# One hybrid attention layer on one core: the transposes of the differential heads' values write to another PSUM pool

## The chip, the core and the metric

The kernel runs on one core of a Trainium2 chip. The metric is the device time of one execution in microseconds (us). The engines are named as the profile names them: PE (matrix products and transposes), PEld (its weight loads), DVE (vector), ACT (scalar), POOL and SP (which only issues DMAs here). Each takes its own instructions strictly in the order of the program and waits at semaphores for the others. The granted clock of PE was 0.996 of full speed over the profiled execution, which is the 2.4 GHz level throughout.

## What is computed

One decoder layer on 1024 tokens of 1024 features. The input is normalised and projected by one matrix whose columns feed two groups of heads; their gated outputs are concatenated, projected, normalised and added to the input. Cut to what matters here:

```python
h = rmsnorm(x, ln_pre_g)
q_nope, q_rope, c_kv, k_rope, g_a, dq, dk, dv, g_b = split(h @ w_in)
# group A: 4 heads over a shared latent c_kv (normalised, then up-projected to keys and values)
o_a = causal_attention(q_a, k_a, v_a, 192 ** -0.5) * silu(g_a)
# group B: 4 differential heads; dq, dk are two maps of 64, dv is 128 wide
a1 = causal_attention(rope(dq)[..., 0, :], rope(dk)[..., 0, :], dv, 64 ** -0.5)
a2 = causal_attention(rope(dq)[..., 1, :], rope(dk)[..., 1, :], dv, 64 ** -0.5)
o_b = rmsnorm(a1 - lam * a2, subln_g) * (1 - lambda_init) * silu(g_b)
x = x + rmsnorm(concat(o_a, o_b) @ w_out, ln_post_g)
```

The projections are made transposed (features on partitions, 512 tokens at a time). The attention needs the values with tokens on partitions, so each head's values are transposed back after their projection. That step is what the change touches.

## The kernel before

Every fp32 product is split in a high and a low half and done in three passes (high by high, high by low, low by high).

The **projection** of one 128-column tile for 512 tokens is 24 matrix products of 512 columns (L512) into one bank of the pool `psj` (tile name `j`, two banks), over eight slices of the input `xh`, `xl` with weights `wh`, `wl`. `ORDER` (L952) lists which tile comes when: for the differential heads the gates `gb`, keys `dk`, queries `dq` and values `dv`, then the latent `c`, the shared rotary key `kr` and the rest. After each tile a generator takes the result out of its bank: `ev_g`, `ev_dk`, `ev_dq`, `ev_c`, and `ev_dv` for the values. Rotary tiles leave the bank by two DVE instructions (L263, a shuffle, and L264). The latent `c` keeps its bank through a long chain: ACT copy, transposes (L283), squares, a power on POOL, a scaling on DVE (L292 to L300), transposes back (L309) and the last evictions (L310, L311).

The **attention** of one head and one pair of query blocks is two stages. `stage1` makes the scores (L698) in 512-column pieces in the pool `pss` (tile `s`, two banks), and DVE copies each piece out, masks it and takes its minimum (L704); ACT makes the exponentials (L711). For the differential heads the two maps are combined by DVE (L729, odd query blocks) or by ACT and POOL (L733, L734, even ones). `stage2` transposes the probabilities on PE (L761) into the pool `pst` (tile `t`, two banks), splits them in two halves by ACT (L111) and DVE (L112) and multiplies them with the values (L774, L779) into `pso` (tile `o`, two banks). `finish_b` normalises a head's output (L819 to L839, among them L833 on PE).

Sets of the two stages are merged with the projection: after each piece of attention, `pump` lets the projection's generator run for a share of that time, so the projection's products fill PE while DVE and ACT work on scores. This gives the order in which the work is written. The Tile framework then puts each engine's instructions in a static order of its own, from that order, the dependencies and the banks: the banks of a pool go round in the order in which the tiles are asked for, and a tile can be written only when the tile two before it in its pool has been read for the last time. So two things tie PE to DVE: a score piece waits for L704 of the piece two before, and a projection tile waits for the last read of the tile two before.

`ev_dv` for heads 1 to 3 (head 0's call has `have_r=False`, made at the start from the first products): DVE scales the bank into `e` (L424); after a pause of two steps four PE transposes (L435) write `e` back into the same bank `ps`; ACT and DVE then split that bank into `dvh` and `dvl` (L437, recorded under the helper's lines L111 and L112). The bank of `psj` is thus held until the second of these has read it. For head 0 the transposes already go to a bank of `pst`.

Of the kernel before, what the change touches and what calls it, by code (L numbers as in the profile page):

```python
# [8 lines left out]
F32 = mybir.dt.float32  # L9
# [7 lines left out]
P = 128  # L17
# [34 lines left out]
def hybrid_layer_kernel(  # L52
# [29 lines left out]
    pst = ctx.enter_context(tc.tile_pool(name="pst", bufs=2, space=PSUM))  # L82
# [27 lines left out]
    def split(hi, lo, src, eng=None):  # L110
        nc.scalar.copy(hi, src)  # L111
        (eng or nc.vector).tensor_tensor(lo, src, hi.bitcast(F32), op=ALU.subtract)  # L112
# [305 lines left out]
    def ev_dv(ps, n, h, have_r=True):  # L418
        cs = slice(n * 512, (n + 1) * 512)
        if n == 0:  # L420
            state["dv", h] = hin.get("dvh"), hin.get("dvl")
        if have_r:
            e = tp.tile([P, 512], F32, tag="e", name="e")
            nc.vector.tensor_tensor(e, ps, R[:, cs], op=ALU.mult)  # L424
        else:
            slot = hin.get("dve", F32)
            hin.put(slot)
            e = slot[0][:, 0:512]
            nc.scalar.copy(e, ps)
            yield  # L430
            nc.vector.tensor_tensor(e, e, R[:, cs], op=ALU.mult)
        yield
        pt = ps if have_r else pst.tile([P, 512], F32, tag="t", name="t")
        for j in range(4):
            nc.tensor.transpose(pt[:, j * P : (j + 1) * P], e[:, j * P : (j + 1) * P], ident)  # L435
        v = state["dv", h]
        split(v[0][0][:, cs], v[1][0][:, cs], pt)  # L437


    evict = {  # L440
        "c": (ev_c, 4), "kr": (ev_kr, 2), "qn": (ev_qn, 2), "qr": (ev_qr, 2), "ga": (ev_g, 0),
        "dk": (ev_dk, 4), "dq": (ev_dq, 2), "dv": (ev_dv, 2), "gb": (ev_g, 0),
    }
    ready = set()
# [218 lines left out]

    tab = load_tables(1)
    gens = [ev_dv(acc[2][n], n, 0, False) for n in range(2)]
    for n in range(2):
        next(gens[n])
# [385 lines left out]
```

## Time and profile before

| | us |
|---|---|
| median of three runs | 598.85 |
| lowest, highest | 598.53, 599.79 |
| the profiled execution | 598.69 |
| its span, first to last instruction | 596.6 |
| outside the span | 2.1 |
| busy in the span: PE | 582.9 (98%) |
| busy in the span: DVE | 352.8 (59%) |
| busy in the span: ACT | 299.9 (50%) |
| busy in the span: POOL | 264.0 (44%) |

A share of the span hides that DVE is used unevenly. From 260 to 290 us it is busy for 28.3 us of 30, and from 310 to 320 us for 2.7 of 10. A busy PE isn't a PE at its peak either: a product's record is longer than the distance to the next, since they overlap.

### The profile page before, as it was taken

The page shows a single profiled execution, that of the slowest core. Times are in us where ns is not written, and L with a number is a line of the kernel's source. Part 1 is how long each engine was busy: PE and PEld are TensorE (multiplying, and loading weights), DVE is VectorE, ACT ScalarE, POOL GpSimd, SP SyncE. Part 2 cuts the span into 40 slices and gives each one's busy share as a digit, 9 for nine tenths or more (in the row PEclk, how much of TensorE's full clock was granted, in tenths as well). Part 3 has the DMA queues.
Part 4 walks back from the last instruction along what each step waited for, and adds up shares of the span by engine and source line. Part 5 has one row for each costly group of instructions (what it writes and reads, how often), then busy time and mean ns, then how long its engine had stood idle before and what let it go on. Part 6 is the DMA issues. An engine that isn't in the chain of part 4 may idle for free.

```text
span 596.6 us, 9022 instructions
## 1 busy us (share of the span) xinstructions
PE 582.9 (98%) x3072; PEld 494.8 (83%) x3072; DVE 352.8 (59%) x893; ACT 299.9 (50%) x682; POOL 264.0 (44%) x246
## 2 busy tenths in 40 slices
PE   8999999999999999999999999999999999999995
PEld 5887888788788888887888888888888878888885
DVE  4459566865678585789963555454346477345232
ACT  5743445555555544577643555454445875333111
POOL 2455884393685769538856222014310870000000
PEclk9999999999999999999999999999999999999998
DMA  8943981144041545201125110012403541443223
GB/s 291 404 147 86 215 230 46 44 117 105 26 107 35 131 111 158 63 27 45 47 60 124 37 53 19 34 47 66 113 27 107 169 144 45 139 155 109 70 71 106
DMA packets 39901, 61.60 MB, mean 103 GB/s; under 512 B 4784, under 2 KB 17328, under 8 KB 39856
## 3 DMA queue, kind: packets, MB, share of 16 engines
q1 hardware_dynamic: 39712, 61.03, 34.7%
q8 instruction: 24, 0.39, 0.3%
q14 instruction: 21, 0.17, 0.1%
q10 hardware_dynamic: 144, 0.01, 0.0%
HBM read 38.47 MB, written 7.86 MB: 78 GB/s over the span
## 4 chain that ended last, share of the span: by engine, by line
PE 81%; DVE 8%; DMA 5%; issue 2%; ACT 2%; POOL 1%; SPq 1%; DVEq 0%; POOLq 0%; ACTq 0%
PE j L512 40%; PE j L599 15%; PE s L698 11%; PE o L774 6%; PE t L761 5%; DMA xn<-in_x_dram 2%; DMA xr<-in_xT_dram 1%; DVE pr L704 1%; DMA wor<-in_wout_dram 1%; PE o L779 1%; PE j L358 1%; DMA wf<-in_w_dram 1%; PE j L492 1%; PE o L806 1%; DVE pl L112 1%
## 5 line engine op out<-in xcount | busy, mean ns | idle before, releaser
L512 PE MATMUL j<-xh,wh 128*128 128x512 f32 x368 | 147.2, 400 | 1.6 <-DVE e L264 0.9
L512 PE MATMUL j<-xl,wh 128*128 128x512 f32 x368 | 145.4, 395 | 0.0
L512 PE MATMUL j<-xh,wl 128*128 128x512 f32 x368 | 145.4, 395 | 0.0
L711 ACT ACTIVATE pr<-pr,st 128x128 f32<-128x128 f32 (+7 forms) x96 | 74.5, 776 | 71.2 <-DVE st L704 65.3
L129 POOL TENSOR_TENSOR wl<-wr,wh 128x512 fp32r<-128x512 f32 x48 | 63.4, 1320 | 70.1 <-ACT wh L128 70.1
L512 PEld LDWEIGHTS j<-xh,wh 128*128 128x128 f32 x368 | 69.3, 188 | 14.2 <-DVE e L264 1.3
L512 PEld LDWEIGHTS j<-xh,wl 128*128 128x128 f32 x368 | 69.2, 188 | 13.0
L512 PEld LDWEIGHTS j<-xl,wh 128*128 128x128 f32 x368 | 69.3, 188 | 11.8
L704 DVE CUSTOM_DVE_ANT_0 pr<-s,mask 128x512 f32<-128x512 f32 (+3 forms) x96 | 54.2, 569 | 34.3 <-PE s L698 30.2
L112 DVE TENSOR_TENSOR pl<-t,ph 128x512 fp32r<-128x512 f32 (+1 forms) x80 | 45.5, 578 | 20.0 <-ACT ph L111 19.1
L111 ACT CAST ph<-t 128x512 fp32r<-128x512 f32 (+1 forms) x80 | 38.5, 495 | 29.7 <-PE t L761 29.5
L761 PE MATMUL t<-ident,pr 128*128 128x128 f32 x288 | 48.2, 273 | 1.9 <-DVE pr L729 1.5
L599 PE MATMUL j<-woh,mh 128*128 128x512 f32 (+1 forms) x119 | 45.5, 384 | 0.0
L599 PE MATMUL j<-wol,mh 128*128 128x512 f32 (+1 forms) x119 | 45.1, 379 | 0.0
L599 PE MATMUL j<-woh,ml 128*128 128x512 f32 (+1 forms) x119 | 44.9, 379 | 0.1
L128 ACT CAST wh<-wr 128x512 fp32r<-128x512 f32 x48 | 29.6, 617 | 25.3 <-PE j L512 17.0
L761 PEld LDWEIGHTS t<-ident,pr 128*128 128x128 f32 x288 | 35.6, 141 | 7.6 <-ACT dvh L111 1.3
L108 POOL TENSOR_TENSOR q<-q,nhalf 128x1 f32<-128x1 f32 x8 | 4.4, 552 | 82.7 <-DVE q L610 82.7
L704 DVE CUSTOM_DVE_ANT_0 pr<-s,mask,st 128x256 f32<-128x256 f32 (+2 forms) x48 | 27.8, 580 | 16.2 <-PE s L698 14.8
L698 PE MATMUL s<-dkh,dq 128*128 128x512 f32 (+2 forms) x96 | 34.7, 363 | 0.8 <-DVE st L704 0.6
L265 POOL TENSOR_TENSOR sw<-sw,sr 128x512 f32<-128x512 f32 x18 | 23.2, 1291 | 23.6 <-DVE sw L263 23.5
L698 PE MATMUL s<-dkl,dq 128*128 128x512 f32 (+2 forms) x96 | 32.7, 342 | 0.0
(218 smaller groups left out, 1296.7 us busy)
## 6 DMA issues: line engine op xcount, KB each, us to landing
wr<-in_wt_dram SPq DMA_DIRECT2D x50, 256.0 KB, 2.7
xn<-in_x_dram SPq DMA_DIRECT2D x8, 512.0 KB, 9.6
dkh<-kh SPq DMA_DIRECT2D x32, 128.0 KB, 2.6
dkl<-kl SPq DMA_DIRECT2D x32, 128.0 KB, 2.6
wor<-in_wout_dram SPq DMA_DIRECT2D x16, 256.0 KB, 3.2
xn<-in_x_dram SPq DMA_DIRECT2D x16, 256.0 KB, 3.9
xr<-in_xT_dram SPq DMA_DIRECT2D x7, 512.0 KB, 6.8
scratch<-og SPq DMA_DIRECT2D x28, 128.0 KB, 1.8
```

Of the source, the lines that this page charges most:

```text
L111: nc.scalar.copy(hi, src)
L112: (eng or nc.vector).tensor_tensor(lo, src, hi.bitcast(F32), op=ALU.subtract)
L128: nc.scalar.copy(wh[:, :w], raw[:, :w])
L129: (eng or nc.gpsimd).tensor_tensor(wl[:, :w], raw[:, :w], wh[:, :w].bitcast(F32), op=ALU.subtract)
L265: nc.gpsimd.tensor_tensor(sw, sw, tab[1][:, cs], op=ALU.mult)
L512: nc.tensor.matmul(ps, a[:, c], b[:, n * 512 : (n + 1) * 512], start=(k == 0 and pi == 0), stop=(k == KT - 1 and pi == len(passes) - 1),)
L599: nc.tensor.matmul(ps[:, :w], a[u], wo[k][v][:, cs], start=(i == 0 and pi == 0), stop=(i == KT - 1 and pi == 2))
L698: nc.tensor.matmul(s[:, :wm], a[:, qb * P : (qb + 1) * P], b[:, c0 : c0 + wm], start=(pi == 0), stop=(pi == len(passes) - 1),)
L704: nc.vector.tensor_tensor_reduce(pr[:, c0 : c0 + w], s[:, :w], m_, -scale, 3e38 if mx is None else mx, ALU.add, ALU.min, mx2)
L711: nc.scalar.activation(pr[:, :n], pr[:, :n], AF.Exp, bias=mx, scale=-1.0, accum_out=l)
L761: nc.tensor.transpose(pt[:, i * P : (i + 1) * P], b[0][:, b[1] * P : (b[1] + 1) * P], ident)
L774: nc.tensor.matmul(o[:, 0:256], a[:, ks], b[:, i * 256 : (i + 1) * 256], start=(g == 0 and i == 0 and pi == 0), stop=False,)
```

## The change

One expression. The four transposes of each 512 values of heads 1 to 3 (six sets, 24 transposes) write to a fresh tile of `pst`, the pool of the probabilities' transposes, and no longer to the projection's own bank. No instruction is added or dropped; the split reads `t` in place of `j`.

```diff
@@ ev_dv @@
         yield
-        pt = ps if have_r else pst.tile([P, 512], F32, tag="t", name="t")
+        pt = pst.tile([P, 512], F32, tag="t", name="t")
         for j in range(4):
             nc.tensor.transpose(pt[:, j * P : (j + 1) * P], e[:, j * P : (j + 1) * P], ident)
```

The bank of `psj` is free after L424 then, and the values' tiles stand in the round of `pst` between the probabilities' tiles. The framework's order comes out differently from the first set on (about 100 us into the run), for about 1,100 of PE's instructions; from about 330 us, in the attention of the first group A head, PE's order is the same again to the end. Three places follow.

**First place, PE, where the values of head 1 used to be transposed.** `dkh_447`, `dkl_448` and `dq_468` are keys and queries of the first head. Before:

```order
L512 MATMUL j<-xh_124,wl 128x512
L698 MATMUL s<-dkh_447,dq_468 128x512
L698 MATMUL s<-dkl_448,dq_468 128x512
L833 MATMUL o<-ss,sel 128x8
L698 MATMUL s<-dkh_447,dq_468 128x384
L698 MATMUL s<-dkl_448,dq_468 128x384
L435 MATMUL j<-ident,e 128x128 x4
L761 MATMUL t<-ident,pr 128x128 x6
```

Now:

```order
L512 MATMUL j<-xh_123,wl 128x512
L512 MATMUL j<-xh_124,wh 128x512
L512 MATMUL j<-xl_132,wh 128x512
L761 MATMUL t<-ident,pr 128x128 x6
L512 MATMUL j<-xh_124,wl 128x512
L512 MATMUL j<-xh_117,wh 128x512
L512 MATMUL j<-xl_125,wh 128x512
```

The second set of head 1's transposes stood right ahead of six transposes of probabilities. Now projections stand around these six, and the set itself comes at row 606 of PE's order in place of row 463, the first set at row 576 in place of row 437.

**Second place, PE and DVE, between the first and the second differential head.** `dkh_724` to `dkl_727`, `dq_942` and `dq_943` belong to the second head, whose first score pieces are made here. On PE, before, some of these pieces, and among them the six transposes:

```order
L512 MATMUL j<-xh_119,wh 128x512
L761 MATMUL t<-ident,pr 128x128 x6
L512 MATMUL j<-xl_127,wh 128x512
L512 MATMUL j<-xh_119,wl 128x512
L512 MATMUL j<-xh_120,wh 128x512
L512 MATMUL j<-xl_128,wh 128x512
L512 MATMUL j<-xh_120,wl 128x512
L512 MATMUL j<-xh_121,wh 128x512
L698 MATMUL s<-dkh_726,dq_943 128x256
L698 MATMUL s<-dkl_727,dq_943 128x256
```

On PE, now, all of them:

```order
L698 MATMUL s<-dkl_450,dq_469 128x512
L761 MATMUL t<-ident,pr 128x128 x2
L698 MATMUL s<-dkh_724,dq_942 128x256
L698 MATMUL s<-dkl_725,dq_942 128x256
L698 MATMUL s<-dkh_726,dq_943 128x256
L698 MATMUL s<-dkl_727,dq_943 128x256
L698 MATMUL s<-dkh_724,dq_942 128x256
L698 MATMUL s<-dkl_725,dq_942 128x256
L698 MATMUL s<-dkh_726,dq_943 128x256
L698 MATMUL s<-dkl_727,dq_943 128x256
L833 MATMUL o<-ss,sel 128x8
L761 MATMUL t<-ident,pr 128x128 x6
```

On DVE, now, beside them, up to the third of the four pieces of 256 columns. Ahead of the first row stand L704 of the last 512-column piece of the first head (`s<-dkl_450,dq_469` above) and L704 of the first short piece:

```order
L820 SCALAR_TENSOR_TENSOR og<-o,gsub,g 128x256
L828 STREAM_TRANSPOSE sx<-sq 128x256
L704 ISA pr,st<-s,mask 128x128
L704 ISA st 128x1
L830 TENSOR_REDUCE ss<-sx 128x8
L723 RECIPROCAL st<-ls 128x1
L831 TENSOR_TENSOR ss<-ss,fn 128x8
L724 TENSOR_SCALAR st<-st 128x1
L729 SCALAR_TENSOR_TENSOR pr<-pr,st 128x512 x2
L723 RECIPROCAL st<-ls 128x1
L835 TENSOR_SCALAR r_1269<-o 128x8
L704 ISA pr,st<-s,mask 128x256
```

The projections that stood between these score pieces are gone from there (they come earlier). On PE no product of the projection stands from row 534 to row 583; the next after row 551 above is at row 584. Behind the six transposes comes a score piece of 384 columns, which needs the bank that the last row of DVE above frees.

**Third place, PE and DVE, at the latent's tiles.** `dkh_2253`, `dq_2673` before and `dkh_2257`, `dq_2677` now are the same keys and queries of the fourth differential head. On PE, before:

```order
L698 MATMUL s<-dkh_2255,dq_2674 128x512
L698 MATMUL s<-dkl_2256,dq_2674 128x512
L512 MATMUL j<-xh_121,wl 128x512
L512 MATMUL j<-xh_122,wh 128x512
L512 MATMUL j<-xl_130,wh 128x512
L512 MATMUL j<-xh_122,wl 128x512
L512 MATMUL j<-xh_123,wh 128x512
L512 MATMUL j<-xl_131,wh 128x512
L512 MATMUL j<-xh_123,wl 128x512
L512 MATMUL j<-xh_124,wh 128x512
L512 MATMUL j<-xl_132,wh 128x512
L512 MATMUL j<-xh_124,wl 128x512
```

On PE, now, the same score piece and what follows it:

```order
L698 MATMUL s<-dkh_2259,dq_2678 128x512
L698 MATMUL s<-dkl_2260,dq_2678 128x512
L774 MATMUL o<-ph,dvh_2066 128x256
L774 MATMUL o<-ph,dvl_2067 128x256
L698 MATMUL s<-dkh_2257,dq_2677 128x384
L698 MATMUL s<-dkl_2258,dq_2677 128x384
L774 MATMUL o<-pl,dvh_2066 128x256
L779 MATMUL o<-pf,vf 128x128
L761 MATMUL t<-ident,pr 128x128 x3
L698 MATMUL s<-dkh_2257,dq_2677 128x256
L698 MATMUL s<-dkl_2258,dq_2677 128x256
L698 MATMUL s<-dkh_2259,dq_2678 128x384
```

Six rows on (the second product of that piece, a transpose, two L774 and a score piece of 256 columns) and up to five rows ahead of the next projection (the rest of the last piece here, another of 256 columns, two L774):

```order
L774 MATMUL o<-pl,dvh_2836 128x256
L698 MATMUL s<-dkh_2257,dq_2677 128x512
L698 MATMUL s<-dkl_2258,dq_2677 128x512
L779 MATMUL o<-pf,vf 128x128
L761 MATMUL t<-ident,pr 128x128
L698 MATMUL s<-dkh_2257,dq_2677 128x256
L698 MATMUL s<-dkl_2258,dq_2677 128x256
L833 MATMUL o<-ss,sel 128x8
L283 MATMUL j<-ident,ce 128x128 x4
L309 MATMUL j<-ident,ce 128x128 x4
L761 MATMUL t<-ident,pr 128x128 x5
L698 MATMUL s<-dkh_2259,dq_2678 128x512
```

On DVE, now, beside this second piece, from one 256-column score piece to the next of 512:

```order
L704 ISA pr,st<-s,mask,st 128x256
L704 ISA st 128x1
L831 TENSOR_TENSOR ss<-ss,fn 128x8
L724 TENSOR_SCALAR st<-st 128x1
L300 TENSOR_SCALAR ce<-j,c_3146 128x128 x4
L729 SCALAR_TENSOR_TENSOR pr<-pr,st 128x512
L723 RECIPROCAL st<-ls 128x1
L292 TENSOR_TENSOR c_3332<-rstd 128x4
L820 SCALAR_TENSOR_TENSOR og<-o,gsub,g 128x256
L835 TENSOR_SCALAR r_3022<-o 128x8
L704 ISA pr,st<-s,mask 128x512
```

Ten projections of the latent's second tile that stood behind the score piece are gone from there; with the bank of the last values free sooner they come earlier. Now 35 rows of PE's order follow each other without a product of the projection (rows 1200 to 1234), and the two banks of `psj` hold the two tiles of the latent meanwhile.

## Rows read from the trace of the kernel before

**Rows 1.** The page: busy time of each engine.

```profile
PE 582.9 (98%) x3072; PEld 494.8 (83%) x3072; DVE 352.8 (59%) x893; ACT 299.9 (50%) x682; POOL 264.0 (44%) x246
```

**Rows 2.** Busy by stretch: us, PE (x), PEld (x), DVE (x), ACT (x), POOL (x), clock.

```profile
98.00:300.00 202.00, 198.22 (x1078) 168.85 (x1078) 150.12 (x428) 116.65 (x292) 131.12 (x122) 1.00 0.29 77
```

**Rows 3.** PE in order of time, two breaks: start, length, [idle before, releaser].

```profile
107.74 0.84 PE L761 MATMUL t<-ident,pr 128*128 128x128 f32 x6 [1.05 <-DVE pr L729]
...
164.33 0.51 PE L512 MATMUL j<-xh,wh 128*128 128x512 f32 x1 [0.86 <-DVE e L264]
```

**Rows 4.** PE in order of time, stretches without a break.

```profile
100.27 0.60 PE L435 MATMUL j<-ident,e 128*128 128x128 f32 x4
100.62 0.48 PE L512 MATMUL j<-xh,wh 128*128 128x512 f32 x1
100.94 0.40 PE L512 MATMUL j<-xl,wh 128*128 128x512 f32 x1
101.17 0.40 PE L512 MATMUL j<-xh,wl 128*128 128x512 f32 x1
...
110.25 0.28 PE L774 MATMUL o<-ph,dvh 128*128 128x256 f32 x1
110.37 0.28 PE L774 MATMUL o<-ph,dvl 128*128 128x256 f32 x1
...
282.39 0.33 PE L698 MATMUL s<-dkh,dq 128*128 128x384 f32 x1
282.56 0.34 PE L698 MATMUL s<-dkl,dq 128*128 128x384 f32 x1
```

**Rows 5.** DVE in order of time at the latent's tiles.

```profile
262.12 0.76 DVE L297 TENSOR_TENSOR c<-c,rstd 128x4 f32<-128x4 f32 x1
262.92 1.13 DVE L300 TENSOR_SCALAR ce<-j,c 128x128 f32<-128x128 f32 x4
263.96 0.68 DVE L704 CUSTOM_DVE_ANT_0 pr<-s,mask 128x512 f32<-128x512 f32 x1
...
264.57 0.48 DVE L820 SCALAR_TENSOR_TENSOR og<-o,gsub,g 128x256 f32<-128x256 f32 x1
264.97 0.43 DVE L828 STREAM_TRANSPOSE sx<-sq 128x256 f32<-128x256 f32 x1
265.32 0.77 DVE L292 TENSOR_TENSOR c<-rstd 128x4 f32<-128x4 f32 x1
266.01 0.41 DVE L112 TENSOR_TENSOR pl<-t,ph 128x256 fp32r<-128x256 f32 x1
266.35 0.40 DVE L830 TENSOR_REDUCE ss<-sx 128x8 f32<-128x256 f32 x1
266.67 0.15 DVE L723 RECIPROCAL st<-ls 128x1 f32<-128x1 f32 x1
266.79 0.17 DVE L831 TENSOR_TENSOR ss<-ss,fn 128x8 f32<-128x8 f32 x1
266.87 0.21 DVE L724 TENSOR_SCALAR st<-st 128x1 f32<-128x1 f32 x1
267.00 0.55 DVE L704 CUSTOM_DVE_ANT_0 pr<-s,mask 128x384 f32<-128x384 f32 x1
...
267.47 1.56 DVE L729 SCALAR_TENSOR_TENSOR pr<-pr,st 128x512 f32<-128x512 f32 x1
268.95 0.47 DVE L704 CUSTOM_DVE_ANT_0 pr<-s,mask,st 128x256 f32<-128x256 f32 x1
...
280.07 0.48 DVE L704 CUSTOM_DVE_ANT_0 pr<-s,mask,st 128x256 f32<-128x256 f32 x1
```

**Rows 6.** DVE by line and form: busy us, mean ns of one, idle before.

```profile
L729 DVE SCALAR_TENSOR_TENSOR pr<-pr,st 128x512 f32<-128x512 f32 x16 | 15.3, 978 | 0.2
L704 DVE CUSTOM_DVE_ANT_0 pr<-s,mask 128x128 f32<-128x128 f32 x12 | 3.4, 286 | 9.5 <-PE s L698 9.3
```

**Rows 7.** PEld's waits: line, tile, releaser, us in total, times, longest.

```profile
PEld t L761 <- ACT dvh L111: 1.3, 1, 1.3
```

## The prediction

> **What bounds the kernel now.** PE is busy for 98% of the span [rows 1], and nothing else is near that, so I read the profile in this order: the share of each engine, then PE's busy time by stretch, then PE's own records in order of time, to see where it stood still. From 98 to 300 us, the stretch in which the change lets instructions move, PE lacks 202.0 - 198.2 = 3.8 us of full use, DVE is busy for 150 of 202 us and no other engine for more [rows 2]. The 3.8 us are six breaks and some slivers: 1.05 us at 107.7 (six transposes of probabilities wait for L729 on DVE), 0.60 and 0.86 us near 163 (a score piece waits for L704, a projection for L264), and 0.41, 0.23 and 0.47 us from 269 to 278. Two of them are shown [rows 3]. A break costs more than its record of idle time. A product of 512 columns is recorded as 0.40 us long but the next starts after 0.23 us [rows 4], so 0.17 us of the record before the break is lost too, and after it some 0.10 us in the restart. Six breaks are 3.8 + 6 x 0.27 = **5.4 us**. That is all that a better order of these instructions could give back. Before 98 us and after about 330 us PE's order stays as it is.
>
> **The prices.** On PE, from start to start [rows 4]: 0.23 us for 512 columns, 0.17 for 384, 0.12 for 256. Four transposes take 0.35 us, and the product behind them needs 0.32 where 0.23 is usual, so they cost 0.44, or 0.11 each; L779 and L833, fp32 in two passes, are taken as two transposes, 0.22. On DVE [rows 5] an instruction starts about 0.08 us before the record of the one ahead of it ends, so its price is its record less 0.08: L704 of 512 columns 0.61, of 384 0.47, of 256 0.40; L820 0.40, L828 0.35, L830 0.32, L112 of 256 0.34, L723 0.12, L831 0.08, L724 0.13, L835 as L831, four L300 1.04. L704 of 128 columns is 0.29 - 0.08 = 0.21, and L729 of 512 columns has a mean of 0.98, so 0.90 [rows 6]. The record of 1.56 us in the excerpt shows that it can be 1.48. The four-element instructions of the latent (L292, L293, L294, L297) lie between 0.08, as L831 with its eight elements, and 0.80, which is L297 here; I take the middle, 0.44.
>
> The Trainium skill ("VectorE: DVE Perf Modes", section "The DRAIN you can't avoid") says that the next DVE instruction doesn't start until the pipeline of the one before is empty, unless nothing holds it. If records really followed each other end to end, the two sums of DVE below, of 14 and 27 instructions, would be 1.1 and 2.2 us longer and the time 606.0. The excerpt shows L828 starting 0.40 us into the 0.48 us of L820 [rows 5], so the row decides here.
>
> **Part 1: what it removes.** The bank of `psj` is no longer held over the pause, the four transposes, ACT's copy and DVE's subtraction. So projections can go earlier, and in the new order they do: around the six transposes that waited at 107.7 stand projections now (first place), and the score pieces of the second differential head that stood together at 161 to 164 are apart. The breaks near 270 lie in a piece that is rebuilt altogether. I take off all six: **-5.4 us**. The work itself is unchanged: same transposes, same two evictions, reading another bank.
>
> **Part 2: what it moves.** The projections that were pulled forward are missing later. They were what PE did while DVE and ACT worked on the scores. Two stretches are left in which PE has only attention, and there the rule holds that a score piece can start only when L704 of the piece two before has ended. So from the end of one score piece to the start of a later one, PE needs at least what DVE's queue holds between the two L704, in its order, whatever PE itself has to do.
>
> *Second place.* From the last 512-column piece of the first head to the 384-column piece of the second. PE has 2 transposes, 8 products of 256, L833 and 6 transposes: 0.22 + 0.96 + 0.22 + 0.66 = 2.1 us. DVE has, from L704 of that piece to L704 of the third 256-column piece: 0.61, two of 128 columns 0.42, L820 0.40, L828 0.35, L830 0.32, two L723 0.24, L831 0.08, L724 0.13, two L729 1.80, L835 0.08, and 0.40: 4.8 us. PE stands for **2.7 us**. With L729 at the price of the nearest other 512-column row, 0.61, it is 2.2; with both at 1.48 it is 3.9.
>
> *Third place.* From the piece of 512 columns with which the first excerpt of the new order begins, to the one of 256 columns just ahead of the next projection. PE has 5.7 us: six score pieces in between (three of 256, two of 384, one of 512 columns: 0.72 + 0.68 + 0.46) and a second product pair of 512 at the end (0.46), six L774 (0.72), two L779 and L833 (0.66), 18 transposes (1.98). DVE has seven L704 (two of 512, two of 384, three of 256: 3.36), two L820 0.80, L828 0.35, L112 0.34, L830 0.32, two L723 0.24, L831 0.08, two L724 0.26, four L300 1.04, L729 0.90, L835 0.08: 7.8 us, and four of the four-element kind, 1.8: 9.5 us. PE stands for **3.8 us**. With the four-element ones at 0.08 and L729 at 0.61 it is 2.1; with 0.80 and 1.48 it is 5.9.
>
> The same pricing can be tested on the kernel before. From its L704 at 263.96 to that at 280.07 DVE has 40 instructions, which it prices at 15.2 us; the trace shows 16.1 us from start to start [rows 5], and 0.6 of the difference is the slow L729 among them.
>
> To these come the edges of two breaks, 2 x 0.35 us (0.17 and 0.10 as above, and 0.08 for the last DVE record, which must end): **+0.7 us**.
>
> *What this count doesn't see.* It holds only for DVE's queue between score pieces. On the kernel before it finds one place, 0.7 us at 161 to 164 where the trace lost 2.0 in two breaks, and nothing at 107.7, where 1.3 were lost to probabilities that came late. So breaks by other chains will be there in the new order too. Most of the old ones are inside the two places that are counted above, so I add less than the 4.7 us that it misses before: **+2.0 us**, between 0.5 and 4.5.
>
> *Covered at no cost.* The values come later: the second set of head 1 stands at row 606 of PE's order, and its first reader is at row 630, with three transposes, two products of 384 and some twenty of 512 between, over 5 us; ACT's copy and DVE's subtraction, each 512 columns wide as the 0.68 us of L704 [rows 5], fit into that even behind another eviction. If DVE is behind by more, the next head's L774 wait. And the values' tile now stands in the round of `pst`, so a tile of probabilities behind it waits for its two evictions. Head 0 does that already before the change, and PE's weight loads waited for its `dvh` once, 1.3 us [rows 7]; three such waits, one for each head, would be 4 us. I count them in the 0.5 to 4.5 above.
>
> **The sum.** -5.4 + 2.7 + 3.8 + 0.7 + 2.0 = +3.8 us on the profiled execution's 598.69 (a span of 596.6 and 2.1 around it): 602.5. The median of the runs is 0.16 above that execution, so **602.7 us**. The bounds are -5.4 + 2.2 + 2.1 + 0.7 + 0.5 = +0.1, or 599.0, and -5.4 + 3.9 + 5.9 + 0.7 + 4.5 = +9.6, or 608.5.
>
> **Rivals.**
>
> *The breaks go and nothing takes their place: faster.* The mechanism is the bank of `psj`, free some microseconds sooner at six places, so that PE always finds a projection. It decides if DVE's queue at the two places takes no longer than PE's own work, which means 2.1 in place of 4.8 us and 5.7 in place of 9.5. Against it: the trace has no such DVE prices, and the order shows no projection there. With 2 us of other breaks left it would be 598.9 - 5.4 + 2.0 = 595.5. Chance **0.08**.
>
> *It evens out.* Both places at their lower bounds and few other breaks give 599.0, within 1.2 us of the time before, and a measurement of this kernel can tell about 0.2%, or 1.2 us, from no change. Chance **0.12**.
>
> *DVE is slower there than I price it.* L729 reads two tiles of SBUF while POOL runs, and its record of 1.56 us against a mean of 0.98 [rows 5, 6] shows that something holds it up at just this kind of place. With the upper prices the two places give 3.9 and 5.9 us, and with 2.0 of other breaks the time is 598.9 - 5.4 + 9.8 + 0.7 + 2.0 = 606.0. Chance **0.25**. The Trainium skill ("SBUF — State Buffer", section "Who interferes with whom") states that a DVE instruction with two inputs in SBUF contends with a POOL instruction that reads SBUF. The long record agrees with it, though no row here shows it to be the cause.
>
> *The values' tiles hold up the probabilities.* Three waits as in [rows 7] on top of the forecast: 602.7 + 3 x 1.3 = 606.6. For it: the round of two banks. Against it: `e` is ready long before, so the tile is taken only for two evictions. Chance **0.10**.
>
> My forecast, the sum as it stands, has **0.45**.
>
> **How the numbers follow.** Slower by over 0.2% (above 600.05) holds the forecast and the last two rivals: 0.80. The same: 0.12. Faster: 0.08. The range of 8 in 10 goes from 599.0, which leaves out the faster case and half of the even one, to 607.5, a little below the upper bound, since not all of the upper prices should come together.
>
> **What would show it.** PE's timeline should have no break at the six transposes of the first place. It should show breaks of 2 to 4 us in all ahead of the second head's first 384-column piece, released by L704 or L729, at about 120 us, and of 2 to 6 us between the latent's second tile and the next projection, at about 260 to 272 us, with DVE busy all through both. PE's idle time from 98 to 330 us should rise from under 4 to 7 us or more, and after that the two traces should run in step, shifted by the same amount. The forecast is wrong if DVE stands idle in these two places, if the breaks are elsewhere (at L774 waiting for `dvh`, at L761 waiting for a bank), or if PE's idle time doesn't rise.

## The result and the profile after

| | before | after |
|---|---|---|
| median on the same chip, us | 599.23 | **604.79** |
| lowest, highest | 598.53, 599.79 | 604.56, 605.48 |
| the profiled execution | 598.69 | 604.56 |
| its span | 596.6 | 602.4 |

The change makes the kernel **slower by 0.92%** (ratio 1.0092, 95% interval 1.0077 to 1.0107), 5.6 us. The busy shares, the answer to [rows 1], hardly tell: PE did the same work and was busy for 97% of a longer span.

```profile
PE 586.0 (97%) x3072; PEld 497.9 (83%) x3072; DVE 355.7 (59%) x893; ACT 300.4 (50%) x682; POOL 266.2 (44%) x246
```

The window of [rows 2] doesn't tell it either: PE lacks 4.5 us of full use where it lacked 3.8, and DVE's busy time is nearly the same. The one new thing is the clock in the column behind POOL, 0.99 in place of 1.00.

```profile
98.00:300.00 202.00, 197.51 (x1064) 168.84 (x1063) 151.10 (x424) 116.38 (x290) 130.65 (x119) 0.99 0.29 77
```

So I counted PE's time in another way. From each PE instruction I took the distance to the start of the next one, less the median distance of its kind in the kernel before (its columns, and whether it is a transpose, a two-pass fp32 product or another), and summed this by stretch. Breaks, their edges and slow clocks are all in it. The sums add up to the difference of the spans: 5.75 us for 5.8.

| lost time against before, us | 98–115 | 115–132 | 132–200 | 200–255 | 255–280 | 280–300 | 300–315 | rest | sum |
|---|---|---|---|---|---|---|---|---|---|
| the change | -2.4 | +3.1 | -2.2 | 0.0 | +4.1 | +0.6 | +2.1 | +0.5 | +5.8 |

This is the whole case in a row. The change takes away the break at 107 us [rows 3] and the two near 163 us, as predicted. It pays with breaks at the second place (115 to 132 us) and at the third (from 255 us), also as predicted, and with one at 304.7 us that I hadn't named. After 315 us the two traces run in step. Of the +0.5 in the column "rest", 0.4 lies ahead of 98 us, where the order is still the same: that is the difference of two executions and not of the change.

**Second place.** PE and DVE in order of time (start, length, then in brackets the idle time before and what ended it):

```profile
123.64 0.29 DVE L704 CUSTOM_DVE_ANT_0 pr<-s,mask 128x128 f32<-128x128 f32 x1
123.78 0.39 PE L698 MATMUL s<-dkh,dq 128*128 128x256 f32 x1 [0.41 <-DVE st L704]
123.85 0.48 DVE L820 SCALAR_TENSOR_TENSOR og<-o,gsub,g 128x256 f32<-128x256 f32 x1
124.24 0.43 DVE L828 STREAM_TRANSPOSE sx<-sq 128x256 f32<-128x256 f32 x1
124.60 0.25 DVE L704 CUSTOM_DVE_ANT_0 pr<-s,mask 128x128 f32<-128x128 f32 x1
124.92 0.39 PE L698 MATMUL s<-dkh,dq 128*128 128x256 f32 x1 [0.41 <-DVE st L704]
...
125.56 1.42 DVE L729 SCALAR_TENSOR_TENSOR pr<-pr,st 128x512 f32<-128x512 f32 x2
126.47 0.85 PE L761 MATMUL t<-ident,pr 128*128 128x128 f32 x6 [0.62 <-DVE pr L729]
127.04 0.41 DVE L704 CUSTOM_DVE_ANT_0 pr<-s,mask 128x256 f32<-128x256 f32 x1
127.51 0.44 PE L698 MATMUL s<-dkh,dq 128*128 128x384 f32 x1 [0.20 <-DVE st L704]
```

DVE has an instruction in hand all through, and each of PE's four breaks ends with an L704 or L729.

**Third place.** PE, DVE and ACT:

```profile
263.49 0.21 DVE L724 TENSOR_SCALAR st<-st 128x1 f32<-128x1 f32 x1
263.59 0.71 ACT L711 ACTIVATE pr<-pr,st 128x512 f32<-128x512 f32 x1
264.55 0.58 ACT L111 CAST dvh<-t 128x512 fp32r<-128x512 f32 x1
265.01 0.28 ACT L767 COPY pf<-t 128x128 f32<-128x128 f32 x1
265.16 0.69 DVE L112 TENSOR_TENSOR dvl<-t,dvh 128x512 fp32r<-128x512 f32 x1 [1.46 <-ACT dvh L111]
265.44 0.46 PE L779 MATMUL o<-pf,vf 128*128 128x128 f32 x2 [0.88 <-ACT pf L767]
266.05 0.69 DVE L704 CUSTOM_DVE_ANT_0 pr<-s,mask 128x512 f32<-128x512 f32 x1
266.80 0.39 PE L698 MATMUL s<-dkh,dq 128*128 128x256 f32 x1 [0.57 <-DVE st L704]
...
274.43 0.48 DVE L704 CUSTOM_DVE_ANT_0 pr<-s,mask,st 128x256 f32<-128x256 f32 x1
```

Here DVE stands still for 1.46 us at the subtraction of head 3's values, because ACT makes their cast behind an exponential and some squares. Then its queue takes from 266.05 to 274.8 us, 8.8 us, with one wait of 0.34 us for ACT in it, where I had counted 5.7 us of work for PE.

**Fourth place**, which I had not seen in the order. PE, DVE and POOL:

```profile
303.32 2.43 DVE L729 SCALAR_TENSOR_TENSOR pr<-pr,st 128x512 f32<-128x512 f32 x2
303.42 1.78 POOL L129 TENSOR_TENSOR wl<-wr,wh 128x512 fp32r<-128x512 f32 x1 [0.33 <-ACT wh L128]
305.67 0.43 DVE L838 STREAM_TRANSPOSE sx<-r 128x256 f32<-128x256 f32 x1
306.03 0.65 DVE L360 TENSOR_TENSOR e<-j,R 128x512 f32<-128x512 f32 x1
306.73 0.50 PE L512 MATMUL j<-xh,wh 128*128 128x512 f32 x1 [1.74 <-DVE e L360]
```

A projection waits for its bank, whose last reader L360 is in DVE's queue behind two L729 that take 2.43 us. The same pair took 1.42 us at 125.56, so about 1.0 of the 1.74 us is the pair's longer record beside POOL (see the last section).

### The profile page after: what moved, and what is told of

Its sections match the earlier page's. It is cut to its first block, busy times and chain, and to the rows that moved or that the text cites. A ratio compares the mean times of both kernels' runs of the same rounds, so it can differ in the third digit from the quotient of the medians.

```text
span 602.4 us, 9012 instructions
## 1 busy us (share of the span) xinstructions
PE 586.0 (97%) x3072; PEld 497.9 (83%) x3072; DVE 355.7 (59%) x893; ACT 300.4 (50%) x682; POOL 266.2 (44%) x246
## 4 chain that ended last, share of the span: by engine, by line
PE 79%; DVE 7%; DMA 6%; issue 3%; ACT 2%; POOL 1%; SPq 1%; DVEq 0%; ACTq 0%; POOLq 0%
PE j L512 38%; PE j L599 15%; PE s L698 11%; PE o L774 7%; PE t L761 4%; DMA xn<-in_x_dram 2%; DMA xr<-in_xT_dram 1%; PE o L779 1%; DMA wor<-in_wout_dram 1%; DMA wf<-in_w_dram 1%; DVE pr L704 1%; PE o L806 1%; PE j L492 1%; PE j L358 1%; DVE pr L729 1%
## 5 line engine op out<-in xcount | busy, mean ns | idle before, releaser
L129 POOL TENSOR_TENSOR wl<-wr,wh 128x512 fp32r<-128x512 f32 x48 | 64.1, 1336 | 69.7 <-ACT wh L128 69.3
L704 DVE CUSTOM_DVE_ANT_0 pr<-s,mask 128x512 f32<-128x512 f32 (+3 forms) x96 | 54.2, 568 | 33.8 <-PE s L698 31.0
L112 DVE TENSOR_TENSOR pl<-t,ph 128x512 fp32r<-128x512 f32 (+1 forms) x80 | 45.1, 579 | 25.1 <-ACT ph L111 24.4
L108 POOL TENSOR_TENSOR q<-q,nhalf 128x1 f32<-128x1 f32 x8 | 4.4, 553 | 82.6 <-DVE q L610 82.6
L704 DVE CUSTOM_DVE_ANT_0 pr<-s,mask,st 128x256 f32<-128x256 f32 (+2 forms) x48 | 27.7, 576 | 18.1 <-PE s L698 16.7
```

The lines of the kernel that those rows point to most:

```text
L129: (eng or nc.gpsimd).tensor_tensor(wl[:, :w], raw[:, :w], wh[:, :w].bitcast(F32), op=ALU.subtract)
L704: nc.vector.tensor_tensor_reduce(pr[:, c0 : c0 + w], s[:, :w], m_, -scale, 3e38 if mx is None else mx, ALU.add, ALU.min, mx2)
```

## Experiments

In each, the kernel before ran on the same chip beside it (medians 598.9 to 599.8). "Queue theory" is the prediction's: PE loses time where it has attention alone and DVE's queue between score pieces is longer than PE's work. The lost time by stretch is that of one profiled execution of each kernel, which can lie up to 2 us from the median beside it.

### Each head by itself

```diff
-        pt = pst.tile([P, 512], F32, tag="t", name="t")
+        pt = ps if have_r and h != 1 else pst.tile([P, 512], F32, tag="t", name="t")
```

and the same with 2 and with 3.

> Only the first differential head after head 0 (h = 1) has its values' transposes in the bank of the probabilities; heads 2 and 3 keep the projection's own bank. The order of PE is that of the changed kernel up to the second head's values, some way past 150 us, and another one after that. Queue theory (PE loses time where it has attention alone and DVE's queue between two score pieces is longer than PE's own work): the old breaks at 107 and 163 us are gone (4.6 us less), the second place at 120 to 130 us costs the same 3.1 to 3.4 us as in the changed kernel, and at the latent's tiles, near 265 us, DVE has 4.9 us between two score pieces where PE has 2.9, so about 2 us there. Sum 599.2 - 4.6 + 3.1 + 2.0 and about 1 for the rest: 600.5, between 599 and 602. Bank theory (each head whose values go through the round of two banks costs the same, because probabilities wait for the values' evictions): a third of 5.6 us, 601.1, with waits of transposes of probabilities for the values' evictions and no loss at 120 us by score pieces that wait for DVE.

> Only head 2 has its values' transposes in the bank of the probabilities. PE's order is that of the kernel before up to head 2's values. Queue theory: the breaks at 107 and 163 us stay, there is no second place at 120 us, and near 265 us DVE's queue exceeds PE's work by only about 1 us, as much as the kernel before lost there: 599.2, between 598 and 600.5. Bank theory: a third of 5.6 us, 601.1.

> Only head 3 has its values' transposes in the bank of the probabilities. PE's order is that of the kernel before up to head 3's values, and then over the latent's tiles that of the changed kernel. Queue theory: the breaks at 107 and 163 us stay (2.2 and 2.3 us), none at 120, and the stretch from 260 to 310 us loses what it loses in the changed kernel, 9.3 us where the kernel before lost 2.9; so this third of the change costs more than the whole: 599.2 + 6.4 = 605.6, between 603.5 and 607. Bank theory: a third of 5.6 us, 601.1.

| | us | ratio, 95% | 98–115 | 115–132 | 132–200 | 200–255 | 255–280 | 280–300 | 300–315 |
|---|---|---|---|---|---|---|---|---|---|
| head 1 only | 600.85 | 1.0021 (1.0010 to 1.0033) | -2.4 | +3.1 | -2.3 | +0.1 | +2.1 | +0.1 | +0.1 |
| head 2 only | 600.35 | 1.0014 (1.0001 to 1.0026) | 0.0 | 0.0 | +1.5 | +0.6 | -0.2 | +1.0 | 0.0 |
| head 3 only | 606.64 | 1.0121 (1.0101 to 1.0142) | 0.0 | 0.0 | 0.0 | 0.0 | +3.6 | +0.9 | +2.2 |

The places separate by head. Head 1 pays for the two old breaks with the second place, and loses a little. Head 3 gains nothing and pays for the third and fourth place, so a third of the change costs more than the whole, by some 1.8 us. An equal price for each head, 601.1 three times, is out. (The row of head 2 comes from its longest execution, 602.45 us; its granted clock was 0.50 from 166 to 168 us, and that is the 1.5 us there.)

### Other banks, and the projection's bank held as before

`bank_o` takes a tile of the outputs' pool for the values. `hold_j` keeps the change and adds one read of the projection's bank behind the split:

```diff
-        pt = pst.tile([P, 512], F32, tag="t", name="t")
+        pt = pso.tile([P, 512], F32, tag="o", name="o") if have_r else pst.tile([P, 512], F32, tag="t", name="t")
```

```diff
-        split(v[0][0][:, cs], v[1][0][:, cs], pt)
+        split(v[0][0][:, cs], v[1][0][:, cs], pt); have_r and nc.vector.tensor_copy(e[:, 0:1], ps[:, 0:1])
```

> The values' transposes of heads 1 to 3 go to a bank of the attention's outputs (pool pso) in place of one of the probabilities' transposes. PE's order is that of the changed kernel nearly to the latent's tiles. Queue theory: the same 3.1 to 3.4 us at 120 to 130 us, and at the latent's tiles DVE's queue exceeds PE's work by 6.7 us by the same prices that gave 4.8 for the changed kernel: 604.8 + 1.9 = 606.7, between 604.5 and 608. Bank theory: the probabilities' banks are not touched, so the time falls back to 599.2 to 601.

> The changed kernel with one more copy on DVE, of one column of the projection's bank behind the two evictions of the values, so that the bank stays held as long as in the kernel before, while the values' transposes stand in the round of the probabilities' transposes as after the change. Theory that the freed bank is the cause (it lets the scheduler move projections): with the bank held again the projections stay late and the time is that of the kernel before within 1 us, 599.3 (598.3 to 600.5). Theory that any new order loses where attention stands alone: by the prices used before, DVE's queue exceeds PE's work by 4.0 us near 110 us and 3.8 us at the latent's tiles in this order, as much as the 7.8 us counted for the change: 604.8 (603 to 606.5). Theory of the round of two banks: 604.8 too, but with transposes of probabilities that wait for the values' evictions in place of score pieces that wait for L704.

`bank_o`: 605.78 us, ratio 1.0103 (1.0079 to 1.0128; executions from 603.62 to 607.67), with +2.9 at the second place, +3.5 from 255 to 280 and +4.0 from 300 to 315 us. Of the last, about 1.7 are products at a granted clock of 0.50 from 306 to 309 us, behind a break of 1.44 us. So a loss of this size doesn't need the probabilities' banks. The count of DVE's queue was right on the sign and wrong on the place: it gave the third place 1.9 us more than the change, and that place lost less.

`hold_j`: 606.87 us, ratio 1.0132 (1.0112 to 1.0151), a little above the range of 603 to 606.5. This was a surprise for the reading that the freed bank is the cause. With the bank held again the order isn't that of before: the projections stand in yet other places, and the lost time is +1.4 and +3.6 us between 98 and 132 and +3.6 between 255 and 300 us. The longest of PE's waits in sum (line, tile, releaser, total, times, longest) are of the same kind as after the change, score pieces that wait for L704; the two behind it, one of them for POOL, are others:

```profile
PE s L698 <- DVE st L704: 3.9, 6, 1.1
PE t L761 <- POOL pr L734: 1.4, 1, 1.4
PE j L512 <- DVE cTl L311: 1.3, 1, 1.3
```

So it is not the bank as such: an edit that holds it, and so makes the framework put the projections elsewhere again, also leaves DVE and PE alone with each other.

### The three places one by one

At the second place, the two L729 of head 0's last query block on 128 of 512 columns (the rest of these columns is left out):

```diff
-                            cs = slice(c0, min(n, c0 + 512))
+                            cs = slice(c0, min(n, c0 + (128 if (hd, p) == (4, 3) else 512)))
```

> The changed kernel with the last two L729 of the first head's last pair (query block 7) done on 128 of their 512 columns; the other columns are left out, so this run only tells about time. These are the two L729 of the second place (1.42 us together in the changed kernel's trace). PE's order there is the same but for three of six transposes that go 11 rows earlier; after 135 us the order differs. Queue theory (PE waits there because DVE's queue is longer than its own work): two L729 of 128 columns, taken as the 0.29 us of L704 of 128 columns, shorten DVE's queue by 0.9 us, and PE's idle time from 115 to 132 us falls from 1.69 to 0.8 (0.5 to 1.1). If PE waits there for something else (the exponentials of ACT, a bank of the scores), it stays within 0.2 of 1.69. The whole time then falls by about as much, 604.8 to 603.9, if the new order after 135 us is as good as the old one; the count of DVE's queue at the latent's tiles is 4.2 us in place of 4.8 there, so 602.5 to 604.5.

603.27 us, ratio 1.0066 (1.0049 to 1.0083), but PE's idle time from 115 to 132 us did not fall: 1.77 us. The two L729 took 0.62 us in place of 1.42, and the 384-column piece that ended the break at 127.51 came at 126.53. With 0.18 us that this trace is ahead anyway, that is 0.8 us won, as expected. Three microseconds later it was gone again:

```profile
129.91 0.16 DVE L723 RECIPROCAL st<-ls 128x1 f32<-128x1 f32 x1 [0.67 <-ACT pr L711]
130.11 0.21 DVE L724 TENSOR_SCALAR st<-st 128x1 f32<-128x1 f32 x1
130.36 0.48 DVE L729 SCALAR_TENSOR_TENSOR pr<-pr,st 128x256 f32<-128x256 f32 x1
130.76 0.68 DVE L112 TENSOR_TENSOR pl<-t,ph 128x512 fp32r<-128x512 f32 x1
131.50 0.38 PE L774 MATMUL o<-pl,dvh 128*128 128x256 f32 x1 [0.59 <-DVE pl L112]
```

The framework had put another L729 ahead of the subtraction `pl`, behind a wait for ACT. The place is longer than I had drawn it, and PE has no projection in it to wait with. The price of L729 is right; that shortening it would bring time is not shown, since the order changed with it. That the whole time fits the expectation (602.5 to 604.5) is no support: from 115 to 132 us this run lost 3.8 us where the change lost 3.1, and what made it shorter is the fourth place, +0.3 in place of +2.1 in the new order.

At the third place, the cast of head 3's values on DVE:

```diff
-        split(v[0][0][:, cs], v[1][0][:, cs], pt)
+        h == 3 and nc.vector.tensor_copy(v[0][0][:, cs], pt); (nc.vector.tensor_tensor(v[1][0][:, cs], pt, v[0][0][:, cs].bitcast(F32), op=ALU.subtract) if h == 3 else split(v[0][0][:, cs], v[1][0][:, cs], pt))
```

> The changed kernel with the cast of head 3's values (dvh) on DVE in place of ACT; the subtraction follows it on DVE. PE's order changes little: at the latent's tiles the first product of pf goes behind three transposes. Theory that DVE's queue stood at the subtraction because ACT's cast of the values came late (in the changed kernel DVE stood idle for 1.46 us there, and PE for 0.88 us at pf): DVE has no such wait any more, the 0.88 us are gone, and PE's idle time from 255 to 280 us falls from 2.54 to about 1.4 although DVE has 1.3 us more to do; the time falls from 604.8 to 603 or so. Theory that only DVE's load counts there: 1.3 us more of it, so PE's idle time rises to 3 us or more and the time to 605.5 to 606.5.

602.73 us, ratio 1.0052 (1.0039 to 1.0066). The time is that of the first theory, the reason isn't. DVE's wait of 1.46 us is gone, yet PE's idle time from 255 to 280 us is 2.88 us, more than the 2.54 of the change. What went is the fourth place (+0.1 in place of +2.1), in another order from 265 us on. What the wait for ACT costs by itself this run doesn't tell. Counted from the L704 of 512 columns ahead of it, the next one comes after 2.99 us in place of 3.70, so PE's first breaks are shorter (0.44 and 0.35 us in place of 0.88 and 0.57). But two instructions on four elements each, L297 and L292, took 0.96 and 1.23 us where the change has 0.14 for both, and PE waits behind the second:

```profile
271.41 1.27 POOL L112 TENSOR_TENSOR cnl<-ce,cnh 128x512 fp32r<-128x512 f32 x1
271.46 1.23 DVE L292 TENSOR_TENSOR c<-rstd 128x4 f32<-128x4 f32 x1
273.15 0.48 PE L698 MATMUL s<-dkh,dq 128*128 128x256 f32 x1 [1.22 <-DVE st L704]
```

So at the third place each break is read from the trace as a wait for DVE or ACT; how much of it is DVE's work, its wait for ACT, or POOL beside it is not taken apart.

At the fourth place, the combination of head 3's last query block by ACT and POOL:

```diff
-                    if qb % 2:
+                    if qb % 2 and (hd, p) != (7, 3):
```

> The changed kernel with the last combination of head 3's two maps (query block 7 of the last pair, the two L729 that took 2.43 us at 303.3 us beside a subtraction L129 on POOL) done as for the even query blocks, by ACT and POOL. The order of all engines is that of the changed kernel up to about 300 us. Theory that the third break (1.74 us at 304.7) is DVE's queue, L729 ahead of L838 and of L360, which frees the projection's bank: without the two L729, L360 can run 2.4 us earlier and the break of 1.74 us and its edges of 0.27 are gone; the time falls from 604.8 by 2.0 to 602.8, between 602 and 603.8. Theory that the break is the bank itself (the projection's bank would come late whatever DVE has ahead of it): PE idle stays at 1.5 us or more between 300 and 315 us and the time at 604.5 to 605.5.

603.20 us, ratio 1.0069 (1.0053 to 1.0085). The order is that of the change up to 300 us, and the break is gone: 0.12 us idle from 300 to 315 us where it was 1.74, the lost time there +0.5 in place of +2.1. The window of this run, with the columns of [rows 2]:

```profile
300.00:315.00 15.00, 14.88 (x73) 12.25 (x73) 10.83 (x21) 7.50 (x13) 12.13 (x9) 1.00 0.16 44
```

This is the cleanest of the runs: one step of DVE's queue taken away and one break less, with the same order up to it. Behind it PE's order changes too, until about 331 us, and the run doesn't part L729's work from its longer record beside POOL.

### Can the count find a faster order?

The same prices of DVE were used on orders with other banks for each head, and with one combination moved from DVE to ACT and POOL.

```diff
 bank_jsj
+        pt = ps if h % 2 else [pst, pss][h // 2].tile([P, 512], F32, tag="ts"[h // 2], name="ts"[h // 2])
 bank_soj
+        pt = [pst, pss, pso, None][h]; tg = "tso"[h % 3]; pt = ps if h == 3 else pt.tile([P, 512], F32, tag=tg, name=tg)
 soj_42: bank_soj, and
-                    if qb % 2:
+                    if qb % 2 and (hd, p) != (4, 2):
 before_42: the kernel before, and the same condition
```

> Head 2's values alone go to another bank, one of the scores' (pool pss), and heads 1 and 3 keep the projection's own. Queue theory: by the prices of DVE that gave 0.7 us for the kernel before and 7.8 for the change, this order has 0.7 us in which DVE's queue is longer than PE's work, so it is the kernel before with the same breaks at 107 and 163 us: 599.3, between 598.3 and 600.3. A theory by which a values' tile in the round of another product costs a bank's wait by itself: a third of 5.6 us, 601.2; in the scores' round it would cost more still, because the scores are what PE waits for.

> Head 1's values go to a bank of the scores (pool pss), head 2's to a bank of the outputs (pool pso), head 3 keeps the projection's own. The breaks at 107 us should go as in the change, since head 1's values no longer hold the projection's bank. Queue theory: by the same prices 1.9 us in all, 0.9 near 120 and 1.0 near 160 us, and none at the latent's tiles, so 599.3 - 5.4 (the six breaks) + 1.9 + 0.7 (edges) + 2.0 (what the count doesn't see) = 598.5, between 597 and 600, and perhaps faster than both kernels. A theory of a price for each values' tile that leaves the projection's bank: two thirds of 5.6 us, 603.

> Head 1's values in a bank of the scores, head 2's in one of the outputs, head 3's in the projection's own, and the odd combination (L729) of head 0's pair 2 by ACT and POOL as the even ones are. By the prices of DVE this order has 0.7 us in which DVE's queue is longer than PE's work, and the break at 107 us should be gone. If the count by DVE's queue were enough: 599.3 - 5.4 + 0.7 + 0.7 + 2.0 = 597.3, faster than both kernels. But the same count gave 598.5 for the banks alone, where 600.0 was measured beside 599.8 of the kernel before; by that miss of 1.5 us it is 599.

> The kernel before, all values in the projection's own bank, with only the odd combination (L729) of head 0's pair 2 done by ACT and POOL. It takes apart what the two edits of the fastest kernel so far did (banks for the values of heads 1 and 2, and this combination; together 596.8 beside 598.9). If the combination alone brings the gain (two L729 less at the break of 107 us): 597 here too. If it needs the order that both give together: by the prices used before, DVE's queue exceeds PE's work by 4.9 us in this order (4.6 of it at the latent's tiles), so 599 + 2 to 4, between 600 and 603.5.

| | us | ratio, 95% | 98–115 | 115–132 | 132–200 | 200–255 | 255–280 | 280–300 | 300–315 |
|---|---|---|---|---|---|---|---|---|---|
| bank_jsj | 601.71 | 1.0037 (1.0025 to 1.0049) | 0.0 | 0.0 | 0.0 | +2.0 | -1.1 | +1.7 | +0.1 |
| bank_soj | 600.04 | 0.9999 (0.9987 to 1.0011) | -2.4 | +4.3 | +0.1 | -0.2 | 0.0 | 0.0 | 0.0 |
| before_42 | 604.46 | 1.0087 (1.0070 to 1.0104) | -1.1 | 0.0 | -0.4 | +1.1 | +4.2 | +0.1 | +1.1 |
| **soj_42** | **596.83** | **0.9965 (0.9951 to 0.9979)** | -2.5 | +2.7 | -2.2 | 0.0 | -1.1 | +0.1 | +0.6 |

`soj_42` beats both kernels: the breaks of 107 and 163 us are gone, as after the change, the third place doesn't appear, and 0.6 us is lost at the fourth. PE's idle time from 98 to 300 us is 1.7 us where it was 3.8 before and 4.5 after the change. 1.4 of it are these four breaks at the second place:

```profile
122.66 0.39 PE L698 MATMUL s<-dkh,dq 128*128 128x256 f32 x1 [0.20 <-DVE st L704]
123.81 0.39 PE L698 MATMUL s<-dkh,dq 128*128 128x256 f32 x1 [0.41 <-DVE st L704]
125.26 0.88 PE L761 MATMUL t<-ident,pr 128*128 128x128 f32 x6 [0.53 <-DVE pr L729]
126.40 0.66 PE L435 MATMUL s<-ident,e 128*128 128x128 f32 x4 [0.26 <-DVE st L704]
```

Neither edit does it alone: the banks give 600.04, the combination 604.46. Of the four forecasts by the count only that of `soj_42` came true (597.3 or, by the earlier miss, 599). `before_42` has the sign, with 604.46 us above its range of 600 to 603.5. `bank_soj` came out just above its range of 597 to 600, but lost 4.3 us near 120, where 0.9 had been counted. `bank_jsj` was expected at 598.3 to 600.3, as the kernel before, and lost 1.9. There DVE stood 4.90 us for a table's DMA at 237.8 us and was late for a score piece at 241.87; that is 0.7 of its +2.0 from 200 to 255 us. The count prices what DVE does, not what it waits for.

## Why the prediction was right, step by step

The forecast was 602.7 us, between 599.0 and 607.5, and slower; measured were 604.79 us. The mechanism was the one named: the projections move ahead, and PE then waits for DVE where it has attention alone.

**What was taken off (-5.4 us).** The old breaks went, and were worth more: 2.4 and 2.2 us at 107 and 163 us, and about 1.8 near 270 us, 6.4 in all. The price of an edge was right: the two breaks near 163 us, of 0.60 and 0.86 us, cost 0.27 and 0.28 us beyond their records. But what I took for slivers near 107.7 us are two short breaks of 0.07 and 0.09 us with edges of their own.

**Second place (+2.7, with its edge 3.05).** Measured 3.1, right where it was said. Two errors cancel. DVE's queue took 4.4 us where I had 4.8 (the pair of L729 cost 1.35 from start to start, not 1.80). And PE stood four times, not once, so the edges are about 1.4 us (3.1 less 1.69 idle), not 0.35, while it stood still for 1.69 us and not 2.7. That the sum fits so well is luck.

**Third place (+3.8, with its edge 4.15): mis-sized.** It lost 4.1 us net of the old breaks there, which are in the first term already, so about 5.9 gross. DVE's queue took 8.8 us with its wait of 0.34, less than the 9.5 counted: the four-element instructions took 0.9 us and not 1.8. What was missing is the break of 0.88 us at `pf` ahead of the first of these L704, which ends with ACT, and the edges of four more breaks. The sign "DVE busy all through" was wrong here (1.46 us idle): part of this place is a wait for ACT, which the prediction left out, and what it costs by itself is open.

**What the count doesn't see (+2.0).** 2.1 us at the fourth place, 0.6 from 280 to 300 us, and 0.4 ahead of 98 us, which is chance: 3.1, within the bounds of 0.5 and 4.5. I had a size for it and no place, so that it covers the fourth place is luck.

**The sum.** -6.4 + 3.1 + 5.9 + 3.1 = +5.7 us for the +3.8 predicted. PE's idle time from 98 to 330 us rose to 6.2 us, short of the 7 I had set as the mark, because more of the loss is edges than I thought. The third place was the term that was off most.

**The rivals.** That nothing takes the breaks' place, and that it evens out, are out. That the values' tiles hold up the probabilities is out: among PEld's waits of 0.2 us and more in the profile after there is none of a `t` for `dvh`, the one of [rows 7] is gone, and `bank_o` is as slow. That DVE is slower than priced was wrong for the two places where I used it, and right at the fourth: there L729 cost 1.2 us, between the mean of [rows 6] and my upper 1.48. At the second place POOL's L129 had ended at 124.25 us, before L729 began; nothing in the prediction had settled that. What stays open is why each order comes out as it does; the runs show only what an order costs.

## What to carry to other kernels

Where a framework sets the order, an edit that touches no work can move the filler: look for the stretches in which the bounding engine is left with work that depends on one other engine, and price that engine's queue between two hand-overs. Here such a count named two of the three places where the change lost time, and the sign. It put the three single heads within their ranges too, but of the last four orders it missed three, so every order must be run: a saved microsecond can be lost again a few microseconds later in a new order. Test one head, one bank or one instruction at a time: here one third of the edit cost more than the whole, and the best version took a different bank for each head, together with one combination moved off DVE.

## What the runs showed of the hardware

**DVE and POOL hold each other up.** An addition of eight elements per partition (L831), whose two inputs are in SBUF, took 0.16 us when POOL read nothing beside it and 2.08 us when it started 0.06 us after a POOL addition of 2.11 us; both ended within 0.03 us of each other. From the trace after:

```profile
296.67 2.11 POOL L734 TENSOR_TENSOR pr<-pr 128x896 f32<-128x896 f32 x1
296.73 2.08 DVE L831 TENSOR_TENSOR ss<-ss,fn 128x8 f32<-128x8 f32 x1
...
270.61 0.16 DVE L831 TENSOR_TENSOR ss<-ss,fn 128x8 f32<-128x8 f32 x1
```

This is no single case: in the traces before and after, 18 records of the small L831, L292, L297 and, with a single tensor as input, L294 are longer than 0.4 us, and each ends within 0.03 us of a POOL instruction beside it. Which one waits can hang on little: the L292 shown at the third place started 0.05 us behind POOL's L112 and took 1.23 us; after the change it started 0.03 us behind the same L112 and took 0.14. L729 goes the same way: two of them 1.42 us with POOL's L129 already done, 2.43 us beside it, and L129 itself 1.78 us there where it took 1.27 at 122.98 beside L704. The record of 1.56 us in [rows 5] began at 267.47 us inside a POOL L129 (267.19 to 268.47) and ended 0.56 us behind it, as the second L729 of the fourth place ended 0.55 us behind its L129. Not every POOL instruction does this: L293, with four elements, took 0.16 us at 274.35 in the middle of a power on POOL (L108, 1.64 us). L820, with one input in PSUM, took 0.48 us at 123.85 beside L129 and 0.47 at 302.93 with POOL idle for part of it. The Trainium skill ("SBUF — State Buffer", section "Who interferes with whom") states that a DVE instruction with two SBUF inputs contends with a POOL instruction that reads SBUF. The rows of L831 and L729 agree, down to the end times. I had cited it in the prediction as a possibility and put no such overlap into the order. At the fourth place it made the break longer; the place itself was missed because the count looks at score pieces only, and there a projection waits for its bank.

**The clock fell after short breaks, and not always at a price.** After the change, from 264 to 268 us, PE was busy for 1.12 and 0.79 us of 2. Then its granted clock fell, and rose again while PE was busy throughout (2 us each; PE busy is the second number, the clock the third from the end):

```profile
264.00:266.00 2.00, 1.12 (x9) 0.88 (x8) 0.76 (x2) 2.00 (x10) 0.02 (x1) 1.00 0.46 131
266.00:268.00 2.00, 0.79 (x6) 0.35 (x3) 1.95 (x6) 2.00 (x8) 1.90 (x3) 1.00 0.00 0
268.00:270.00 2.00, 1.85 (x9) 1.41 (x9) 2.00 (x8) 1.06 (x5) 1.78 (x2) 0.81 0.00 0
270.00:272.00 2.00, 2.00 (x8) 1.81 (x9) 2.00 (x12) 2.00 (x7) 0.53 (x2) 0.50 0.42 131
272.00:274.00 2.00, 2.00 (x17) 1.88 (x16) 2.00 (x8) 1.41 (x8) 1.48 (x3) 0.83 0.02 8
274.00:276.00 2.00, 1.71 (x8) 1.10 (x8) 1.67 (x7) 2.00 (x7) 2.00 (x2) 1.00 0.03 8
```

0.50 is the 1.2 GHz level. The fall isn't fixed by the order: `after_73` has the same order there, was busy for 0.79 and 1.15 us of 2, and stayed at 1.00. It lost as much all the same: from 255 to 300 us 6.9 us in both, counted from full clock. That fits slower products that only fill time in which PE would have waited for DVE. At the second place it does cost: `dvh_dve`, with the order of the change there, had a clock of 0.90 from 115 to 132 us and lost 0.85 us more.
